# The order table of a hybrid decoder layer, made anew: POOL's transfers, VectorE's rows beside POOL's, and TensorE's fp32 runs

## The chip, the core and the metric

The kernel runs on one core of a Trainium2 chip. Its engines are TensorE (PE in the profile; PEld is its weight load), VectorE (DVE), ScalarE (ACT), GpSimd (POOL) and SyncE (SP, which only issues transfers here). Each engine works through one queue of instructions in order; semaphores hold an instruction until what it needs is there. The metric is the device time of one execution in microseconds; several executions give a median.

## The reference, cut to what matters

One post-norm decoder layer over 512 tokens of width 1024, batch 1, all in float32:

```python
h = x @ w_in[l]
y_a = nsa_attention(nsa_q, cmp_k, cmp_v, ...) @ w_nsa_out[l]     # 8 heads of 64, 2 groups, three branches
y_b = gated_deltanet(gdn_qkv, ...) @ w_gdn_out[l]                # 4 heads of 128, chunks of 64
mix = (sigmoid(gate_a) * y_a + sigmoid(gate_b) * y_b) @ w_o[l]
x = layer_norm(ALPHA * x + mix, ln1_g[l], ln1_b[l])
f = (silu(gate) * val) @ w_down[l]                               # gate, val = split(causal_dwconv(x @ w_up, conv_w))
x = layer_norm(ALPHA * x + f, ln2_g[l], ln2_b[l])
```

The compressed branch of the attention takes a softmax over 31 blocks; the selected and the windowed branch are causal softmaxes over 512 keys. The delta rule needs, for each head and chunk, the inverse of a lower triangular 64 x 64 matrix.

## The kernel before

**Tiling.** Activations lie transposed, 128 channels on the partitions and 512 tokens along the row. Every large product is computed on pairs: an operand is split into a rounded half `h` and the rest `l` (both float32r), and `product` (L484, L486, L487) adds three matmuls of 512 columns for each 128 x 128 block of weights: `xh·wh`, `xl·wh`, `xh·wl`. `split_w` loads the weights (`raw`, L463, on SP), rounds them (`wh`, L470 on ScalarE or L472 on another engine) and subtracts (`wl`, L474). Transposes and the small products of the delta rule's inverse are plain fp32 matmuls, so TensorE's queue changes between fp32 and float32r.

**Stages.** The input projection, the two mixers of eight and of four heads, interleaved, come first (to about 335 us), then the merge with its gates (`merge`, `mt` L1121, `pm` products, L1199 and L1201; to about 440 us), the output projection, and the feed-forward part. The names that are needed below:
- `cmp_attn` (L993 to L1020) makes the compressed branch of a group: the scores `cs`, their exponentials (L1007, four on ScalarE), their sums `csm` (L1009 to L1012), the product `cs<-cs,csm` (L1013, VectorE, both inputs in SBUF), and four transposes of it (L659) on TensorE.
- `scores` (L1035 on) makes one unit of a head: two matmuls (L1042, L1043), the masked minimum (L1046, VectorE), the exponential (L1048, ScalarE), the reciprocal (L1050), then the scaling: for some units VectorE's `mn<-mn,gsig` (L1056, one column) and ScalarE's L1057, for others L1059 on VectorE or POOL. `flip` transposes it (L1075) and multiplies by the values (L1089).
- For each head of the delta rule, `gdn_tri` runs a recurrence of 15 steps on VectorE (`xs`, L772 and L773) that ends in `z` (L775), `gdn_inv` (L784 to L829) builds the inverse out of it by small fp32 matmuls, with copies `x`, `ym` and `z` between them; `gdn_mid` scales columns (`grh`, `grl`, L720, L721, and `at`, L743, POOL). The convolution in front of it makes `acc`, `th`, `kq` and `vraw` (L642 to L655).
- `rsqrt` (L525) is a power of few columns on POOL.
- POOL also issues transfers that add up weights in DRAM: `sums_o` (L503, `osum`, 1024 KB each) and `sums` (L513, `wsum`, 2816 KB each).

**What sets the order.** Code, pools and engine choices create the instructions; at the end, `queues` puts each engine's instructions into the order that the table QUEUES writes out by hand. A number in the table is the place at which the instruction was created on its engine; it comes after the one that stands before it in the table:

```python
    for k, runs in QUEUES.items():
        last = None
        for run in runs.split():
            a, _, b = run.partition("-")
            for n in range(int(a), int(b or a) + 1):
                i = made[k][n]
                if last is not None:
                    tc.add_manual_dep(i, last.name, ...)       # NoSync: a place in the queue, no wait
                last = i
```

Of the kernel before, what the change touches and what calls it, by code (L numbers as in the profile page):

```python
# [70 lines left out]
def layout(a):  # L71
# [62 lines left out]
    "PE": """0-9 11-12 10 13-32 41 38 35-37 33 42-43 53 39 34 54 44-45 47-48 40 50-52 49 55 46 65 56-57 66 59-60 58 61-63 67 64  # L134
71-72 77-78 74 68 79 69 89 75-76 73 70 86 90 87 80 83 91 88 98 81-82 107 101 108 99 84 109-110 100 111 85 102 112 95
113-114 96 115 103 116-117 92 118-119 93 120-122 94 97 123-148 155-178 149-153 104-106 154 183-205 207 206 208-220
179-180 221-230 181-182 235-251 259-260 252-254 261 255 262-264 231 265-267 232 302 268-271 256 303 272 257-258 233
273 234 304-305 274-277 306-307 278-282 308 310 309 311 360 283-290 361 388 291-298 362-365 389-391 366 312-313
367-370 392 371-372 314-315 373-374 393 375-377 394 378 395 379-383 396 299-300 397-405 444-446 301 447 416 406-407
417 408-410 418-419 411 420-434 456 435-436 448-449 457 437-439 458 450 316-317 451 320-321 318 322-323 319 459-463  # L140
324-327 464-466 328 332-339 329-330 467 331 468-471 513 472 340-347 473 514 474-475 348-355 476-477 515 356-359 452
384-387 516 478 517 479 501-502 453-455 412-415 518 503 519-521 504 522-526 440-441 527 442-443 723-724 528-529
725-727 530-532 728-729 480 484 481-483 533-534 485 505-506 535-536 730 486 507-508 731-733 487 734-738 751 739
488-489 752 740 490 509 491 741-742 492 541-542 753 493-494 754 743 495 510 496 543 511 546 755 497 544-545 512 547
756-757 498-499 744 758 500 548 759-760 549-551 560-561 761 745 762-765 562 565-566 766 552 767 746 553 768 554 537
555 591-592 563-564 567 538 568-569 539-540 581-582 769 570 593-596 556 597 557 598 558 599-600 770-771 559 571 583
# [1425 lines left out]
```

## Time and profile before

| | |
|---|---|
| median of three runs (lowest to highest) | 833.2 us (832.77 to 833.51) |
| the profiled execution, its own time | 831.55 us |
| its span, first to last instruction | 829.8 us |
| mean granted clock of TensorE | 0.992 of full speed |
| TensorE busy | 809.2 us, 98% of the span |
| VectorE, ScalarE, POOL busy | 602.5, 409.2, 180.5 us |
| share of the chain that ended last: TensorE, VectorE, DMA | 82%, 9%, 4% |

A row of the profile names the engine, the line of the kernel, the operation and the tiles, `out<-in`. Busy time is the time in which an engine executes something; a wait is the idle time in front of an instruction, with what ended it. The clock of TensorE is given as a share of its full 2.4 GHz.

### The profile page before, as it was taken

The page shows a single profiled execution, that of the slowest core. Times are in us where ns is not written, and L with a number is a line of the kernel's source. Part 1 is how long each engine was busy: PE and PEld are TensorE (multiplying, and loading weights), DVE is VectorE, ACT ScalarE, POOL GpSimd, SP SyncE. Part 2 cuts the span into 40 slices and gives each one's busy share as a digit, 9 for nine tenths or more (in the row PEclk, how much of TensorE's full clock was granted, in tenths as well). Part 3 has the DMA queues.
Part 4 walks back from the last instruction along what each step waited for, and adds up shares of the span by engine and source line. Part 5 has one row for each costly group of instructions (what it writes and reads, how often), then busy time and mean ns, then how long its engine had stood idle before and what let it go on. Part 6 is the DMA issues. An engine that isn't in the chain of part 4 may idle for free.

```text
span 829.8 us, 11767 instructions
## 1 busy us (share of the span) xinstructions
PE 809.2 (98%) x4138; PEld 673.8 (81%) x4138; DVE 602.5 (73%) x1339; ACT 409.2 (49%) x912; POOL 180.5 (22%) x176
## 2 busy tenths in 40 slices
PE   9999899999999999999999999999999999999996
PEld 8778688778888888888788898888888888878784
DVE  5656779979868976647549965667577577687897
ACT  4453487765576764513335333435334344574641
POOL 0333805141266111152200111102112101100001
PEclk9999999999999999999999999999999999999999
DMA  8333615134284711334365476333938932466583
GB/s 279 102 92 101 252 32 133 44 96 108 49 219 111 233 51 52 120 108 128 115 241 177 152 147 211 125 102 102 215 103 249 229 102 80 150 199 182 190 257 124
DMA packets 43979, 119.58 MB, mean 144 GB/s; under 512 B 3472, under 2 KB 4624, under 8 KB 43664
## 3 DMA queue, kind: packets, MB, share of 16 engines
q1 hardware_dynamic: 32144, 87.37, 32.3%
q0 software_dynamic: 11776, 31.46, 16.3%
q8 instruction: 33, 0.54, 0.3%
q14 instruction: 26, 0.21, 0.1%
HBM read 116.72 MB, written 33.55 MB: 181 GB/s over the span
## 4 chain that ended last, share of the span: by engine, by line
PE 82%; DVE 9%; DMA 4%; ACT 2%; issue 2%; POOL 1%; ACTq 0%; DVEq 0%; POOLq 0%; SPq 0%
PE pu L484 10%; PE pu L486 10%; PE pu L487 10%; PE gps L484 8%; PE gps L486 8%; PE gps L487 8%; DMA raw<-wsum 3%; PE pw L1288 3%; PE px L1452 3%; PE pu L1288 2%; PE pz L1452 2%; PE pout L1089 2%; PE pu L1452 2%; PE aps L1075 2%; PE pm L484 2%
## 5 line engine op out<-in xcount | busy, mean ns | idle before, releaser
L474 DVE TENSOR_TENSOR wl<-raw,wh 128x512 fp32r<-128x512 f32 x146 | 102.7, 705 | 78.0 <-ACT wh L470 38.6
L470 ACT ACTIVATE wh<-raw 128x512 fp32r<-128x512 f32 x126 | 79.1, 629 | 133.7 <-PE pu L486 97.0
L486 PE MATMUL pu<-ml,wh 128*128 128x512 f32 (+1 forms) x384 | 131.5, 373 | 0.0
L484 PE MATMUL pu<-mh,wh 128*128 128x512 f32 (+1 forms) x384 | 130.8, 372 | 0.4 <-ACT mh L1267 0.4
L487 PE MATMUL pu<-mh,wl 128*128 128x512 f32 (+1 forms) x384 | 130.8, 373 | 0.0
L484 PE MATMUL gps<-xh,wh 128*128 128x512 f32 x320 | 125.7, 404 | 3.2 <-ACT mt L1121 2.1
L486 PE MATMUL gps<-xl,wh 128*128 128x512 f32 x320 | 126.1, 401 | 0.0
L487 PE MATMUL gps<-xh,wl 128*128 128x512 f32 x320 | 124.4, 400 | 0.0
L484 PEld LDWEIGHTS pu<-mh,wh 128*128 128x128 f32 x384 | 71.3, 188 | 13.4 <-ACT mh L1267 0.7
L487 PEld LDWEIGHTS pu<-mh,wl 128*128 128x128 f32 x384 | 71.4, 188 | 13.0 <-DVE wl L474 0.5
L486 PEld LDWEIGHTS pu<-ml,wh 128*128 128x128 f32 x384 | 71.4, 188 | 12.6
L1410 DVE SCALAR_TENSOR_TENSOR fa<-pu,fcw,fa 128x511 f32<-128x511 f32 (+1 forms) x88 | 64.6, 744 | 17.5 <-ACT fa L1407 16.9
L1416 POOL TENSOR_TENSOR fth<-fth,fa 128x512 f32<-128x512 f32 x22 | 30.4, 1387 | 212.6 <-DVE fth L1415 186.3
L484 PEld LDWEIGHTS gps<-xh,wh 128*128 128x128 f32 x320 | 60.4, 190 | 15.1 <-issue 2.5
L487 PEld LDWEIGHTS gps<-xh,wl 128*128 128x128 f32 x320 | 60.8, 190 | 10.9
L486 PEld LDWEIGHTS gps<-xl,wh 128*128 128x128 f32 x320 | 61.0, 191 | 10.2
L1387 ACT ACTIVATE wh<-raw 128x512 fp32r<-128x512 f32 x67 | 40.1, 626 | 41.0 <-DMA raw<-in_down 13.5
L1388 DVE TENSOR_TENSOR wl<-raw,wh 128x512 fp32r<-128x512 f32 x67 | 44.8, 694 | 17.9 <-ACT wh L1387 17.3
L474 POOL TENSOR_TENSOR wl<-raw,wh 128x512 fp32r<-128x512 f32 x30 | 40.1, 1339 | 13.4 <-ACT wh L470 7.9
L525 POOL TENSOR_TENSOR rs<-rs,minus_half 128x1 f32<-128x1 f32 x8 | 7.2, 901 | 161.4 <-DVE rs L1246 161.4
L1407 ACT ACTIVATE fa<-pu,fcw 128x512 f32<-128x512 f32 x44 | 29.7, 680 | 24.8 <-PE pu L487 22.0
L1048 ACT ACTIVATE sc<-sc,mn 128x384 f32<-128x384 f32 (+2 forms) x64 | 35.7, 560 | 10.5 <-DVE mn L1046 10.1
(365 smaller groups left out, 1719.8 us busy)
## 6 DMA issues: line engine op xcount, KB each, us to landing
raw<-in_up SPq DMA_DIRECT2D x44, 512.0 KB, 3.7
raw<-in_wT SPq DMA_DIRECT2D x40, 512.0 KB, 3.6
wsum<-in_down POOLq DMA_DIRECT2D x6, 2816.0 KB, 20.8
raw<-wsum SPq DMA_DIRECT2D x20, 512.0 KB, 3.9
raw<-in_down SPq DMA_DIRECT2D x15, 512.0 KB, 4.3
osum<-in_wo POOLq DMA_DIRECT2D x6, 1024.0 KB, 9.0
wsum<-wsum POOLq DMA_DIRECT2D x2, 2816.0 KB, 14.6
raw<-in_wm SPq DMA_DIRECT2D x8, 512.0 KB, 3.5
```

Source lines behind the costliest of these rows:

```text
L470: A.activation(wh, r, AF.Copy)
L474: eng.tensor_tensor(wl, r, wh.bitcast(F32), op=OP.subtract)
L484: i = PE.matmul(ps, wh[k], mh_(k), start=(k == 0), stop=False)
L486: PE.matmul(ps, wh[k], ml_(k), start=False, stop=False)
L487: PE.matmul(ps, wl[k], mh_(k), start=False, stop=(k == n - 1))
L1048: A.activation(s[:, i, :n], s[:, i, :n], AF.Exp, scale=-1.0, bias=mn[:, 0, i:i + 1], accum_out=mn[:, 1, i:i + 1])
L1288: PE.matmul(ps[t], a[x](j)[:, ts], w[y][:, j % 2, :], start=fresh and j == 0 and i == 0, stop=j == TT - 1 and i == 2, skip_group_check=True)
L1387: A.activation(hi, raw[:, i], AF.Copy)
L1388: V.tensor_tensor(lo, raw[:, i], hi.bitcast(F32), op=OP.subtract)
L1410: V.scalar_tensor_tensor(acc[:, n:], ps[:, :S - n], w[:, i:i + 1], acc[:, n:], op0=OP.mult, op1=OP.add)
L1416: G.tensor_tensor(th, th, g[1], op=OP.mult)
L1452: m = PE.matmul(ps, a[x][:, j, ts], w[y], start=first and i == 0, stop=last and i == 2, skip_group_check=True)
```

## The change

Only the table QUEUES is replaced. The same instructions run on the same engines with the same tiles; what changes is the place of each in the queue of its engine. The new table was made with a limit on the transfers that POOL has in flight, with VectorE's rows kept from POOL's rows that run back to back, and with fp32 runs of TensorE joined. It is two lines shorter, so each line number of the kernel after it is lower by 2 (L1013 becomes L1011).

```diff
 QUEUES = {
-    "PE": """0-9 11-12 10 13-32 41 38 35-37 33 42-43 53 39 34 54 44-45 47-48 40 50-52 49 55 46 65 56-57 66 59-60 58 61-63 67 64
...
+    "PE": """0-9 11-12 10 13-32 41 38 35-37 33 42-43 53 39 34 54 44-45 47-48 40 50-52 46 49 59 62 55 63 65 56 64 60 66-67 61 57-58
...
```

Of TensorE's 3880 matmuls 1529 keep their place; the others move by up to 48 places forward or 55 back. Counted along the queue, the type changes between fp32 and float32r 337 times to reach an fp32 run where it was 359, that is, 11 runs fewer. From about 600 us (in the times of before) all queues are as they were. On SP a handful of transfers move.

The transfers of POOL: wsum1, which was issued at 268 us, now comes first, behind lo (64.9 us) and ahead of gx (68.1 us); osum1 comes at 81 us (was 97.8), wsum0 at 108 (was 80.6), osum0 and the copy to osum2 at about 219. Two issues, the copy to osum3 and the addition to wsum0, now stand ahead of the score scale sc_3056 (234.2 us). The times are those of the neighbours in the trace of before.

**Place A, POOL's queue at 92 to 104 us.** Before: osum1 is the first sum of output weights, grh and grl belong to the next head of the delta rule, vraw is a convolution's result, wl a weight's rest, vm a copy of 32 rows.

```order
L474 TENSOR_TENSOR wl_1362<-raw_1358,wh_1360 128x512
L643 TENSOR_TENSOR acc_1131<-acc_1131,tap_1137 128x509
L1068 CAST vm_111<-vcb_344 32x128
L652 TENSOR_TENSOR th_1140<-th_1140,acc_1131 128x512
L503 DMA osum1_105<-in_wo 512x1x512
L653 TENSOR_TENSOR vraw_1095<-th_1140,acc_1131 128x512
L474 TENSOR_TENSOR wl_1366<-raw_1358,wh_1364 128x512
L720 TENSOR_TENSOR grh_1539<-cst_320,gdh_339 128x512
L1068 CAST vm_111<-vcb_344 32x128
L721 TENSOR_TENSOR grl_1540<-cst_320,gdl_340 128x512
```

The same places after the change:

```order
L472 TENSOR_TENSOR wl_1362<-raw_1358,wh_1360 128x512
L1066 CAST vm_111<-vcb_344 32x128
L641 TENSOR_TENSOR acc_1131<-acc_1131,tap_1137 128x509
L650 TENSOR_TENSOR th_1140<-th_1140,acc_1131 128x512
L718 TENSOR_TENSOR grh_1539<-cst_320,gdh_339 128x512
L651 TENSOR_TENSOR vraw_1095<-th_1140,acc_1131 128x512
L523 TENSOR_TENSOR rn1_655<-ss_654,minus_half_332 128x4
L719 TENSOR_TENSOR grl_1540<-cst_320,gdl_340 128x512
L472 TENSOR_TENSOR wl_1366<-raw_1358,wh_1364 128x512
L501 DMA osum1_105<-in_wo 512x1x512
```

The osum1 issue is gone from here (it comes earlier); the power row rn1_655 now stands between vraw and grl, and wl_1366 behind grl. On ScalarE the four exponentials of cs stood together in front of th_1140; now the third stands behind x_953 and the fourth behind ym_960, copies that wait for the matmuls dps_948 and dps_955.

**Place A, TensorE's queue.** Before, from the last products of one inverse (dps_955, dps_962) to the transposes of cs_1163; gps_1198 and gps_1368 are products of the input projection, dps_1012 and dps_1081 transposes of kq:

```order
L823 MATMUL dps_955<-z_895,m_826 64x64 x4
L487 MATMUL gps_1198<-xh_93,wl_1196 128x512
L484 MATMUL gps_1198<-xh_93,wh_1194 128x512
L487 MATMUL gps_1368<-xh_93,wl_1362 128x512
L828 MATMUL dps_962<-ym_960,x_953 64x64 x4
L659 MATMUL aps_1178<-ident_322,cs_1163 128x128
L659 MATMUL dps_1012<-ident_322,kq_968 128x128 x4
L484 MATMUL gps_1368<-xh_93,wh_1360 128x512
```

After; dps_962 stands four rows ahead of the first of these, with the four transposes dps_1012 and one matmul gps_1198 between:

```order
L485 MATMUL gps_1198<-xh_93,wl_1196 128x512
L485 MATMUL gps_1368<-xh_93,wl_1362 128x512
L482 MATMUL gps_1368<-xh_93,wh_1360 128x512
L484 MATMUL gps_1368<-xl_94,wh_1360 128x512
L485 MATMUL gps_1368<-xh_93,wl_1362 128x512
L482 MATMUL gps_1368<-xh_93,wh_1360 128x512
L484 MATMUL gps_1368<-xl_94,wh_1360 128x512
L485 MATMUL gps_1368<-xh_93,wl_1362 128x512
L657 MATMUL dps_1081<-ident_322,kq_968 128x128 x3
L657 MATMUL aps_1178<-ident_322,cs_1163 128x128
L657 MATMUL dps_1081<-ident_322,kq_968 128x128
L657 MATMUL aps_1178<-ident_322,cs_1163 128x128
```

Two matmuls of gps_1198, seven of gps_1368 and seven transposes of kq now stand between dps_962 and the first transpose of cs, where there was nothing.

**Place B, POOL's queue at 162 to 172 us.** Before; sc_2258 is a unit of scores, wh_2417 to wl_2423 are the halves of one weight:

```order
L1059 TENSOR_SCALAR sc_1586<-sc_1586,mn_1587,gsig_109 128x384
L643 TENSOR_TENSOR acc_1982<-acc_1982,tap_1987 128x510
L768 COPY xs_3094<-cst_320 128x64
L472 CAST wh_2417<-raw_2415 128x512
L503 DMA osum2_106<-osum1_105 512x512
L472 CAST wh_2421<-raw_2415 128x512
L474 TENSOR_TENSOR wl_2419<-raw_2415,wh_2417 128x512
L743 TENSOR_TENSOR at_1558<-at_1558,cst_320 128x512
L1059 TENSOR_SCALAR sc_2258<-sc_2258,mn_2259,gsig_109 128x256 x2
L474 TENSOR_TENSOR wl_2423<-raw_2415,wh_2421 128x512
```

After:

```order
L1057 TENSOR_SCALAR sc_1586<-sc_1586,mn_1587,gsig_109 128x384
L641 TENSOR_TENSOR acc_1982<-acc_1982,tap_1987 128x510
L1057 TENSOR_SCALAR sc_2258<-sc_2258,mn_2259,gsig_109 128x256
L470 CAST wh_2417<-raw_2415 128x512
L1057 TENSOR_SCALAR sc_2258<-sc_2258,mn_2259,gsig_109 128x256
L472 TENSOR_TENSOR wl_2419<-raw_2415,wh_2417 128x512
L741 TENSOR_TENSOR at_1558<-at_1558,cst_320 128x512
L470 CAST wh_2421<-raw_2415 128x512
L718 TENSOR_TENSOR grh_2133<-cst_320,gdh_339 128x512
L472 TENSOR_TENSOR wl_2423<-raw_2415,wh_2421 128x512
```

The score scales moved ahead of the weights' rows and of at_1558; the copy to osum2 and xs_3094 are gone from here.

**Place C, TensorE's queue at 402 to 407 us.** Before; pm1_4617 is the product on which the merge's next mt waits, gps_4659 the product that waits for the buffer of that mt:

```order
L484 MATMUL pm1_4617<-yoh_4005,wh_4599 128x512
L486 MATMUL pm1_4617<-yol_4036,wh_4599 128x512
L487 MATMUL pm1_4617<-yoh_4005,wl_4601 128x512
L487 MATMUL gps_4566<-xh_93,wl_4564 128x512
L484 MATMUL gps_4659<-xh_93,wh_4651 128x512
```

After:

```order
L485 MATMUL pm1_4617<-yoh_4005,wl_4601 128x512
L485 MATMUL gps_4566<-xh_93,wl_4564 128x512
L482 MATMUL gps_4566<-xh_93,wh_4562 128x512
L484 MATMUL gps_4566<-xl_94,wh_4562 128x512
L485 MATMUL gps_4566<-xh_93,wl_4564 128x512
L482 MATMUL gps_4659<-xh_93,wh_4651 128x512
```

The last matmul of pm1_4617 now has four matmuls of gps_4566 behind it, not one, before gps_4659 begins.

**A later place on POOL**, at 244 to 252 us: kq_2802 (245.8 us) now stands behind an osum issue, a copy and the power row so_2607 (248.15 us), with sc_3171 and wl_2969 behind it as before.

## Rows read from the trace of the kernel before

**Rows 1.** The page, part 1: an engine's busy time, its share of the span, its instructions.

```profile
PE 809.2 (98%) x4138; PEld 673.8 (81%) x4138; DVE 602.5 (73%) x1339; ACT 409.2 (49%) x912; POOL 180.5 (22%) x176
```

**Rows 2.** The list of waits of PE (TensorE) over the whole span: engine, what waits and its line, what ended the wait; us in total, times, longest.

```profile
PE aps L659 <- DVE tiny L578: 3.0, 1, 3.0
PE gps L484 <- ACT mt L1121: 2.1, 1, 2.1
...
PE dps L659 <- DVE z L775: 1.3, 1, 1.3
PE aps L1075 <- ACT sc L1057: 1.1, 1, 1.1
```

**Rows 3.** The table by stretches: from and to in us, length, busy time of each engine (instructions), the granted clock of TensorE as a share of full speed, the DMA engines' busy share, GB/s.

```profile
103.00:106.40 3.40, 3.40 (x15) 3.01 (x13) 0.79 (x4) 1.52 (x7) 0.91 (x1) 0.51 0.28 108
171.20:174.70 3.50, 3.50 (x28) 2.42 (x27) 1.89 (x7) 1.42 (x5) 2.09 (x3) 0.51 0.16 29
406.50:410.20 3.70, 3.70 (x11) 2.87 (x10) 3.24 (x7) 2.08 (x4) 0.00 (x0) 0.54 0.45 146
```

**Rows 4.** The timeline of PE in the second of these stretches: start, duration, engine, line, operation, tiles, shapes, count.

```profile
171.56 0.63 PE L1089 MATMUL pout<-pth,vcat 128*128 128x512 f32 x1
171.99 0.64 PE L1089 MATMUL pout<-ptl,vcat 128*128 128x512 f32 x1
```

**Rows 5.** The timeline of PE a little after the first, at the full clock.

```profile
109.14 0.40 PE L486 MATMUL gps<-xl,wh 128*128 128x512 f32 x1
109.37 0.38 PE L659 MATMUL dps<-ident,vraw 128*128 128x128 f32 x2
...
109.83 0.38 PE L659 MATMUL dps<-ident,vraw 128*128 128x128 f32 x2
...
110.28 0.40 PE L486 MATMUL gps<-xl,wh 128*128 128x512 f32 x1
110.52 0.40 PE L484 MATMUL gps<-xh,wh 128*128 128x512 f32 x1
```

**Rows 6.** The answer on line L1013 (shortest, median and longest duration in ns of its two instructions) and the timeline of DVE (VectorE) at the second.

```profile
L1013 DVE TENSOR_TENSOR cs<-cs,csm x2: 684/2600/4516, 98.1 to 216.3; 128x512 f32<-128x512 f32 x2
...
98.12 4.52 DVE L1013 TENSOR_TENSOR cs<-cs,csm 128x512 f32<-128x512 f32 x1
```

**Rows 7.** The timeline of POOL over the same time.

```profile
98.50 1.35 POOL L653 TENSOR_TENSOR vraw<-th,acc 128x512 f32<-128x512 f32 x1
99.74 1.33 POOL L474 TENSOR_TENSOR wl<-raw,wh 128x512 fp32r<-128x512 f32 x1
100.96 1.11 POOL L720 TENSOR_TENSOR grh<-cst,gdh 128x512 fp32r<-128x512 f32 x1
...
102.86 1.05 POOL L721 TENSOR_TENSOR grl<-cst,gdl 128x512 fp32r<-128x512 f32 x1
```

**Rows 8.** The timeline of PE just before its wait for cs.

```profile
99.04 0.67 PE L828 MATMUL dps<-ym,x 64*64 64x64 f32 x8
```

**Rows 9.** The timeline of ACT (ScalarE) before it.

```profile
95.02 0.69 ACT L1007 ACTIVATE cs<-cs 128x128 f32<-128x128 f32 x3
...
98.26 0.38 ACT L825 ACTIVATE ym<-dps 64x256 f32<-64x256 f32 x1 [0.23 <-PE dps L823]
```

**Rows 10.** The timelines of POOL and of DVE at a power row (line L525) elsewhere.

```profile
253.67 1.05 POOL L525 TENSOR_TENSOR rn<-ss,minus_half 128x4 f32<-128x4 f32 x1 [1.53 <-DVE ss L678]
...
253.77 0.68 DVE L474 TENSOR_TENSOR wl<-raw,wh 128x512 fp32r<-128x512 f32 x1
```

**Rows 11.** The timelines of DVE and of POOL before the second fall of the clock.

```profile
166.25 2.54 DVE L1056 TENSOR_TENSOR mn<-mn,gsig 128x1 f32<-128x1 f32 x2
168.72 0.41 DVE L1046 CUSTOM_DVE_ANT_0 sc<-aps,cst 128x256 f32<-128x256 f32 x1
...
166.19 1.29 POOL L474 TENSOR_TENSOR wl<-raw,wh 128x512 fp32r<-128x512 f32 x1
167.42 1.28 POOL L743 TENSOR_TENSOR at<-at,cst 128x512 f32<-128x512 f32 x1
...
170.95 1.11 POOL L1059 TENSOR_SCALAR sc<-sc,mn,gsig 128x256 f32<-128x256 f32 x2 [2.25 <-DVE mn L1050]
```

**Rows 12.** The timeline of all engines before the third, of which three rows are shown.

```profile
403.41 0.39 PE L487 MATMUL pm<-yoh,wl 128*128 128x512 f32 x1
...
405.35 0.60 ACT L1121 ACTIVATE mt<-gps 128x512 f32<-128x512 f32 x1 [8.61 <-DVE mt L1201]
...
406.09 0.47 PE L484 MATMUL gps<-xh,wh 128*128 128x512 f32 x1 [2.06 <-ACT mt L1121]
```

**Rows 13.** The table by stretches once more, at two other places.

```profile
80.00:90.00 10.00, 10.00 (x55) 8.51 (x56) 7.19 (x27) 5.65 (x12) 7.67 (x7) 1.00 0.90 320
140.00:150.00 10.00, 9.98 (x55) 7.94 (x54) 10.00 (x34) 9.36 (x24) 5.13 (x6) 1.00 0.65 198
```

**Rows 14.** The timelines of POOL and of PE at a later power row.

```profile
248.15 1.03 POOL L525 TENSOR_TENSOR so<-so,minus_half 128x4 f32<-128x4 f32 x1 [1.03 <-DVE so L887]
249.60 0.92 POOL L1059 TENSOR_SCALAR sc<-sc,mn,gsig 128x512 f32<-128x512 f32 x1 [0.41 <-DVE so L889]
250.49 1.29 POOL L474 TENSOR_TENSOR wl<-raw,wh 128x512 fp32r<-128x512 f32 x1
...
252.44 0.39 PE L487 MATMUL gps<-xh,wl 128*128 128x512 f32 x1
```

More of the change, by code (lines that the diff above doesn't have):

```diff
@@ L139 @@
[L139 to L143, printed above, removed]
@@ new lines @@
+1460-1462 1457 1463 1472-1473 1398 1483-1485 1399-1401 1486 1402 1487-1488 1474 1464 1501-1502 1465-1466 1475-1476
+1467 1582 1489 1583 1490 1335 1503 1468 1517-1518 1339-1341 1504 1342 1336-1338 1505-1506 1491-1494 1343-1346
+1519-1520 1469 1495 1521 1470 1347-1348 1522 1351-1358 1349 1471 1507-1508 1350 1509-1511 1496-1499 1512-1513
+1359-1366 1523-1524 1544 1500 1545 1584-1585 1546 1367-1374 1525 1514 1547-1550 1610-1611 1515-1516 1586-1588
+1375-1378 1551 1526 1612-1613 1527 1552-1554 1589 1614 1528 1615 1563-1564 1529-1530 1590 1616 1591-1592 1531-1532
@@ new lines @@
+2850-2852 2835 2853 2836 2854-2860 2866 2837 2867 2861 2868 2838 2869 2862 2870 2839-2840 2871-2874 2863 2875 2864
+2841 2876-2878 2865 2879-2881 2890-2891 2882 2892 2883 2893-2902 2884-2886 2903 2914-2915 2904 2916-2917 2887
+2918-2920 2905 2921 2888 2906 2922-2925 2889 2907-2908 2926 2909 2927 2910 2938 2928 2939-2941 2911 2942-2943
+2912-2913 2944 2929 2945-2950 2930-2931 2951 2962 2932 2963 2952 2964-2965 2953-2954 2933 2966 2955 2967-2968 2934
+2969 2935 2970-2971 2936 2972 2956 2973 2957-2959 2937 2960 2986 2974-2975 2987 2961 2976-2978 2988-2991 2979
@@ new lines @@
+3290-3291 3301 3292 3302-3303 3273 3304-3306 3293-3294 3307 3295 3308 3296 3309-3312 3322 3297 3313-3314 3323 3315
+3324-3330 3316-3317 3331-3332 3318 3333-3335 3319 3336 3320 3346 3337-3338 3347 3339-3342 3348-3349 3343-3344
+3350-3352 3345 3353 3370 3354 3321 3355 3371 3356-3361 3372 3362 3373-3379 3363 3380 3364-3365 3381 3366-3367
+3394-3395 3382 3368 3396 3383 3397-3402 3384 3403 3369 3404 3385-3387 3405 3388-3390 3406 3391 3407 3392 3408
+3418-3419 3409 3420 3393 3421-3424 3427 3410 3428 3411 3429 3425 3412 3426 3413 3430-3431 3433-3434 3414 3435 3432
@@ new lines @@
+3821-3825 3849 3826 3850-3851 3827-3828 3852-3853 3829 3854-3855 3830-3836 3856 3837 3857 3838-3842 3858 3843-3844
+3859 3845-3846 3860-3879""",
+    "DVE": """0 27 104 1-4 6 5 7 9 8 10-11 13 12 14 17 15-16 18 58-60 19 61 22 64 20-21 90 65 23 66 62 31 67 32 63 33 25 34 72 35-36
+73 37-54 74 68-69 83 70-71 84 81 91 82 92 55 93 85-87 94 56 88 95 75 80 151 153 29 152 102 30 76-77 28 154 107 57
+109-110 108 89 164 111 165 112 115 96 113 97 114 166-167 116 79 117 98 118-119 99 120 100 121-122 101 123-126 103 127
@@ new lines @@
+37 140 62 26 41 45 54 48 55 42 36 49 51 47 52 64 66 65 67 46 68 57 69 58 50 53 56 59 61 108 104 63 109 75 60 76 80 92
+88 77 81 87 110 144 90 78 84 71-72 106 86 70 73 93 85 74 94 82 91 95 89 96-99 79 100 83 101 111 102-103 112-130 132
+131 133-137 147 138-139 142 150 143 145 153 148 146 149 151-152 154-155 157 156 160 159 158 161 163 162 165 164
+166-171""",
+    "SP": """0-7 17 8-9 15 25 10 12 11 13-14 19 18 16 20-24 26-75 80 79 81-82 78 83 77 84-85 76 86-134 136-165 167 135 169 171
+173-178 168 179-180 172 182 166 170 181 183-184""",
```

365 lines of the change are left out of this document (171 added, 194 removed).

## The prediction, made before the result was known

> **What bounds the kernel now.** I read the page first: TensorE is busy for 809.2 us of the span of 829.8 us [rows 1]. VectorE, the next, is far below that. So the time can fall only where TensorE waits or runs at a lower clock; work taken from another engine counts only if TensorE stood waiting for it. The list of TensorE's waits comes next [rows 2]. It names few long ones: 3.0 us for a row of VectorE (the releaser shown is the small row L578 that ended last; the tile is cs), 2.1 us for `mt` L1121 in the merge, 1.3 us for `z` L775 and 1.1 us for a scaled score L1057. The table by stretches shows what comes behind three of them: in 103 to 106.4, 171.2 to 174.7 and 406.5 to 410.2 us the granted clock is 0.51, 0.51 and 0.54, that is 1.2 GHz for nearly the whole stretch [rows 3]. Before each fall TensorE had waited: 2.97 us, then 1.3 and 1.1 us within seven, then 2.06 us. At the low level two 512-column matmuls start 0.43 us apart [rows 4], at the full one 0.24 us [rows 5], so 3.4 us at the low level do the work of 1.9 us: each fall costs 1.5 us.
>
> **Place A, 96 to 106 us.** VectorE's `cs<-cs,csm` (L1013) starts at 98.12 and takes 4.52 us; the other of its kind takes 0.68 us [rows 6]. Over the same time POOL runs a DMA issue and then vraw, wl_1366 and grh without a gap, and grl after a short copy [rows 7]. VectorE's row ends where the third of these long rows ends. TensorE has finished L828 by 99.7 [rows 8] and has only the transposes of cs in front of it.
>
> The new order does three things here. On ScalarE, two of the four exponentials that L1009 sums now stand behind x_953 and ym_960, one each; all four were over by 95.7, the copy ym ran from 98.26 to 98.64 [rows 9]. Its matmuls are due some 0.4 us sooner, as two products now stand behind them, so the last exponential ends at 98.4 to 98.9. The sum (0.7 us), the reciprocal and two small products bring cs<-cs,csm to a start of 100.0 to 100.5, later than before. On POOL, th_1140 is followed by grh, vraw, and then the power row rn1_655: with their old durations (1.1 and 1.35 us) the power row runs from about 100.3 to 100.9 for 1.05 us. Beside such a row VectorE is not held: a wl with two SBUF inputs took 0.68 us inside one of 1.05 us [rows 10]. So I take it that cs passes in this opening and ends at 101.0 to 101.9. On TensorE nine 512-column matmuls (9 x 0.23) and seven transposes (7 x 0.11) stand between L828 and the first cs transpose, 2.8 us that fill 98.9 to 101.7. A wait of 0 to 0.3 us is left of 2.97: gain 2.7 us, and as a long wait preceded each fall of the clock, 1.5 us more. **A: 4.2 us.** The bounds are 0 (the opening is missed) and 4.5.
>
> The Trainium skill, "SBUF — State Buffer", section "Who interferes with whom", says that a VectorE instruction with two SBUF inputs and a GpSimd instruction that reads SBUF exclude each other, that the one issued first holds the shared ports for its whole length, and that the order of issue decides. This trace agrees that they exclude each other; it differs on the length, since L1013 waited through several rows of POOL, 4.52 us, not one. By that section alone cs would have ended by about 100.5 before the change (vraw's end at 99.85 and its own 0.68 us), and in the changed kernel the power row, which reads SBUF, would hold it too.
>
> **Place B, 160 to 175 us.** `mn<-mn,gsig` (L1056), rows of one column, stands from 166.25 to 168.79 while POOL runs wl_2419 and at_1558 back to back until 168.70 [rows 11]. Now a score scale (sc_2258, L1059) stands ahead of wh_2417, and a second one ahead of wl_2419 and at_1558. It needs extremes (L1046, from 168.72) that come behind L1056 on VectorE, and ran at 170.95. So POOL stands idle when L1056 comes. The scaled score is then some 2.4 us sooner and TensorE's 1.15 us for it go, with 0.2 us right behind: 1.35 us. The pushed-back wl_2419, at 1.3 us a row, still ends before TensorE's work on the stretch 171 to 175 is over. The wait for z ahead of it stays: nothing that VectorE does before z is removed. Whether the clock falls without the second wait I can't read from any row; I put in half of 1.5. **B: 2.1 us**, bounds 0 and 2.9.
>
> **Place C, 403 to 410 us.** From the start of the last pm matmul, 403.41, the chain L1199, L1201, L1121 takes until 406.09 [rows 12], 2.68 us. One matmul covers it now; four will, so three more, 0.7 us. About 1.5 us of waiting are left. Half of the clock's 1.5 again. **C: 1.4 us**, bounds 0.5 and 2.2.
>
> **Joined runs.** Two fp32 runs of two transposes each and three 512-column matmuls fill 109.14 to 110.28, 1.14 us [rows 5]; 4 x 0.11 and 3 x 0.23 make 1.13. A change of type costs under 0.01 us in such a place; the longest step there, 0.32 us from one matmul to the next run, bounds a join at 0.1 us. For 11 joins I take 0.1 us, bounds 0 and 1.
>
> **Transfers.** wsum1 now goes out at 66 us, osum1 at 81 and wsum0 at 108. The stretch 80 to 90, where wsum0 ran and the DMA engines were busy to 0.90, has TensorE at 10.00 of 10 [rows 13]. The loads of SP's queue lie so far ahead there that a slower one is covered; 0, and where the cover fails some tenths for each load. The two POOL issues now ahead of the score scale sc_3056 (about 231 to 238 us) keep it some 3 us longer; TensorE's use moved back by some 2.6 us. Bounds of that: 0 and 1.
>
> **New waits.** Of the 3880 matmuls over 2000 stand elsewhere, moved by up to 55 places, so rows that were in time need not be. One that I walked: behind the power row so_2607 at 248.15 (1.03 us) now stand kq (1.3), the score scale sc_3171 (0.92) and wl_2969 (1.29), which then ends at 252.7; TensorE wants it at 252.44 less one matmul, 252.2 [rows 14]: 0.5 us. Three such places and a part of the bound at sc_3056 make 1.8 us, my estimate; below it lies 0, above it one more place like C, with its fall of the clock, 2.1 + 1.5 us.
>
> **The sum.** 4.2 + 2.1 + 1.4 + 0.1 - 1.8 = 6.0 us off. The profiled execution took 831.55 us for a span of 829.8 us; it lies 1.65 us under the median of the three runs, 833.2 us, which I take as the base: 833.2 - 6.0 = 827.2 us. The other case inside this mechanism is that the clock falls nowhere and no new wait appears: 4.5 + 2.9 + 2.2 + 0.1 = 9.7, so 823.5 us.
>
> **The rivals.**
> - *The opening at A is missed.* If the power row holds VectorE like any other POOL row, or cs comes as grl starts, cs waits through grl and wl_1366 (1.05 and 1.33 us) to 104.3 and, with the osum1 issue behind them, to 105.2. TensorE then waits 2.6 to 3.5 us instead of 2.97, the clock falls again, and the 2.8 us of pulled-forward products are missing behind cs, whose readers come 1.7 to 2.6 us later than now. Against the other terms (at best 2.1 + 1.4 + 0.1 - 1.8 = 1.8 us off, without the halves for the clock 0.3) that gives 833 to 835.5 us. It decides for slower once cs ends after about 105 us. For it speaks the 4.52 us itself; against it the wl beside the power row. That a power row, which reads SBUF, counts like any other follows from the section of the Trainium skill's "SBUF — State Buffer" named above.
> - *A's gain is lost at z.* In 140 to 150 us VectorE is busy for 10.00 of 10 us [rows 13]. If z came no sooner, TensorE would only wait longer at 164 us: A's 4.2 us are lost and 831.2 us are left, with a further new wait 833. Against it: VectorE itself gets 3.8 us back at A and 2.4 at B.
> - *New waits prevail.* Two or three places of C's size (3.6 us each) among the moved rows between 180 and 400 us: 834 to 838 us. For it speaks how many rows move; against it that the stretches with most slack on the other engines are there.
>
> **Chances and range.** The sum 0.50 (824.5 to 830), its better case 0.14 (822 to 824.5), A's gain lost at z 0.17 (831 to 834), the opening missed 0.10, new waits prevail 0.09. A difference under 0.2%, 1.7 us, cannot be told from none. All of the first two, and a little of z, are faster: 0.67. Most of z and a part of the missed opening are the same: 0.14. The rest is slower: 0.19. The range from 822.5 to 834.0 leaves out about one tenth above and less below; the likeliest case alone is 824.5 to 830.
>
> **What would show it.** In the changed profile: L1013 near 0.7 us and no wait of TensorE over 0.5 us for cs; L1056 at 0.15 us and no wait for L1057 near 167 us; a wait for L1121 near 400 us of about 1.5 us; a granted clock of 1.0 right after the cs transposes. The steps fail if L1013 again takes over 2 us, if the wait for z grows by what A saved, or if a low clock stands behind new waits between 180 and 400 us.

## The result, and the profile after

The changed kernel takes 826.43 us (median of 4, 825.69 to 828.08) where the kernel before took 833.36 us (median of 4, 832.77 to 835.01): a ratio of 0.9927, with a 95% interval of 0.9909 to 0.9946, that is 4.5 to 7.6 us faster. Its profiled execution took 826.54 us for a span of 824.8 us, 5.0 us less than the span before. All its line numbers are lower by 2 than those of before.

The page: TensorE is still the bound, and is busy for 3.3 us less [rows 1].

```profile
span 824.8 us, 11773 instructions
PE 805.9 (98%) x4138; PEld 671.2 (81%) x4138; DVE 601.6 (73%) x1339; ACT 409.7 (50%) x912; POOL 181.6 (22%) x176
```

The list of TensorE's waits (what waits, for what; us in total, times, longest):

```profile
PE dps L791 <- DVE ym L788: 2.4, 1, 2.4
PE gps L482 <- ACT mt L1119: 1.5, 1, 1.5
PE gps L555 <- DVE vm L552: 1.4, 1, 1.4
PE dps L657 <- DVE z L773: 1.1, 1, 1.1
PE gps L482 <- issue: 0.9, 1, 0.9
PE aps L1073 <- DVE sc L1057: 0.9, 1, 0.9
PE dps L737 <- DVE yT L893: 0.7, 1, 0.7
```

Against [rows 2]: the 3.0 us for cs and the 1.1 us for the scaled score of L1057 (now L1055) are gone, the wait for `mt` is 1.5 us, that for z is 1.1. A wait of 2.4 us for `ym` is new and now the longest.

The table by stretches (stretch, its length, busy time and count for PE, PEld, DVE, ACT and POOL, granted clock, DMA share, GB/s) shows what comes behind it. The three low stretches of [rows 3] are gone; one is left, at 218.1 us (the clock is low too behind TensorE's last matmul, in every kernel, where it costs TensorE nothing):

```profile
99.00:103.00 4.00, 4.00 (x24) 3.37 (x23) 3.39 (x8) 3.89 (x18) 4.00 (x4) 1.00 0.00 0
218.10:221.60 3.50, 3.50 (x10) 2.63 (x10) 2.08 (x9) 0.88 (x4) 0.00 (x0) 0.51 0.57 106
```

**Place A.** The timeline (start, duration, engine, line, operation) shows VectorE's row and POOL's beside it:

```profile
98.34 1.28 POOL L651 TENSOR_TENSOR vraw<-th,acc 128x512 f32<-128x512 f32 x1
...
99.58 1.05 POOL L523 TENSOR_TENSOR rn<-ss,minus_half 128x4 f32<-128x4 f32 x1
...
99.90 0.69 DVE L1011 TENSOR_TENSOR cs<-cs,csm 128x512 f32<-128x512 f32 x1
...
100.61 1.23 POOL L719 TENSOR_TENSOR grl<-cst,gdl 128x512 fp32r<-128x512 f32 x1
```

The row that took 4.52 us [rows 6] takes 0.69, inside the power row.

**Place B.** The rows of one column, which took up to 2475 ns, stay under 0.2 us (shortest, median, longest in ns):

```profile
L1054 DVE TENSOR_TENSOR mn<-mn,gsig x30: 150/154/193, 109.6 to 313.7; 128x1 f32<-128x1 f32 x30
```

**The new wait, at 212 us.** The timeline of the three engines:

```profile
211.80 1.20 POOL L501 DMA_DIRECT2D osum<-in_wo  x1
...
212.47 1.16 POOL L470 CAST wh<-raw 128x512 fp32r<-128x512 f32 x1
212.48 4.15 DVE L472 TENSOR_TENSOR wl<-raw,wh 128x512 fp32r<-128x512 f32 x1
213.03 1.82 POOL L741 TENSOR_TENSOR at<-at,cst 128x512 f32<-128x512 f32 x1
214.27 1.80 POOL L472 TENSOR_TENSOR wl<-raw,wh 128x512 fp32r<-128x512 f32 x1
...
216.55 0.41 DVE L788 TENSOR_TENSOR ym<-dps,cst 128x256 f32<-128x256 f32 x1
...
217.11 1.08 PE L791 MATMUL dps<-ym,x 128*128 128x64 f32 x8 [2.43 <-DVE ym L788]
```

It is the picture of place A before the change, at another place: a transfer issued by POOL, three rows of POOL behind it, a VectorE row with two SBUF inputs that starts with them and ends 0.56 us behind the last (4.15 us for a row that takes 0.69 elsewhere), and behind it the copy that TensorE wants. So VectorE is held through all three rows of POOL and does its own work after them. TensorE waits 2.43 us and the clock falls.

### The profile page after: what moved, and what is told of

Read it like the earlier page. It is cut to its first block, busy times and chain, and to the rows that moved or that the text cites. A ratio compares the mean times of both kernels' runs of the same rounds, so it can differ in the third digit from the quotient of the medians.

```text
span 824.8 us, 11773 instructions
## 1 busy us (share of the span) xinstructions
PE 805.9 (98%) x4138; PEld 671.2 (81%) x4138; DVE 601.6 (73%) x1339; ACT 409.7 (50%) x912; POOL 181.6 (22%) x176
## 4 chain that ended last, share of the span: by engine, by line
PE 86%; DVE 6%; DMA 3%; ACT 2%; issue 1%; SPq 1%; POOL 0%; DVEq 0%; ACTq 0%
PE pu L484 10%; PE pu L482 10%; PE pu L485 10%; PE gps L482 9%; PE gps L484 9%; PE gps L485 8%; PE px L1450 5%; PE pz L1450 3%; PE pout L1087 2%; PE aps L1073 2%; PE pm L484 2%; PE pm L482 2%; PE pm L485 2%; PE pu L1450 2%; PE dps L657 1%; PE pw L1286 1%
## 5 line engine op out<-in xcount | busy, mean ns | idle before, releaser
L472 DVE TENSOR_TENSOR wl<-raw,wh 128x512 fp32r<-128x512 f32 x146 | 105.8, 728 | 74.0 <-PE pu L485 33.4
L1386 DVE TENSOR_TENSOR wl<-raw,wh 128x512 fp32r<-128x512 f32 x67 | 44.8, 694 | 19.1 <-ACT wh L1385 18.5
```

The source lines that it names most:

```text
L472: eng.tensor_tensor(wl, r, wh.bitcast(F32), op=OP.subtract)
L1386: V.tensor_tensor(lo, raw[:, i], hi.bitcast(F32), op=OP.subtract)
```

## The experiments

Unless said otherwise, each starts from the changed kernel and moves rows of one queue. The ratio is to the kernel before, timed beside it.

| kernel | median us (lowest to highest, n) | ratio, 95% |
|---|---|---|
| changed kernel | 826.43 (825.69 to 828.08, 4) | 0.9927, 0.9909 to 0.9946 |
| a_row_moved | 822.64 (822.27 to 824.41, 4) | 0.9890, 0.9865 to 0.9916 |
| a_no_cover | 829.24 (824.16 to 832.86, 10) | 0.9943, 0.9914 to 0.9972 |
| b_scores_behind | 828.71 (826.14 to 830.24, 8) | 0.9951, 0.9934 to 0.9968 |
| c_cover_back | 828.88 (824.71 to 832.4, 10) | 0.9952, 0.9929 to 0.9975 |
| fix_dve | 822.60 (821.85 to 823.33, 4) | 0.9881, 0.9859 to 0.9904 |
| fix_two | 822.16 (820.37 to 823.10, 4) | 0.9876, 0.9849 to 0.9903 |
| before_b (from before) | 832.54 (829.79 to 835.89, 10) | 0.9994, 0.9969 to 1.0018 |
| transfers_back | 829.11 (827.0 to 830.04, 7) | 0.9958, 0.9943 to 0.9973 |
| before_no_issue (from before) | 825.26 (824.13 to 827.18, 4) | 0.9910, 0.9878 to 0.9942 |
| issue_212 | 822.49 (821.45 to 823.44, 4) | 0.9870, 0.9835 to 0.9905 |
| runs_split | 827.39 (821.68 to 829.26, 10) | 0.9923, 0.9895 to 0.9952 |
| best | 822.28 (821.6 to 823.07, 4) | 0.9867, 0.9850 to 0.9885 |

### The power row taken out of place A (a_row_moved)

```diff
 L501 DMA osum_105<-in_wo 512x1x512
+L523 TENSOR_TENSOR rn_655<-ss,minus_half 128x4
 L472 TENSOR_TENSOR wl<-raw,wh 128x512
...
 L651 TENSOR_TENSOR vraw<-th,acc 128x512
-L523 TENSOR_TENSOR rn_655<-ss,minus_half 128x4
 L719 TENSOR_TENSOR grl<-cst,gdl 128x512
```

> The changed kernel with one row of POOL's queue moved: the power row rn1_655 goes back to where it was (behind the osum1 issue at 79 us), so that vraw, grl, wl_1366 and an osum1 issue run without it between. Theory (the opening at the power row is what frees VectorE): cs<-cs,csm, 0.69 us in the changed kernel, takes 2 to 4 us again, TensorE waits 0.6 to 2.6 us at the first cs transpose (none there in the changed kernel), and the time rises from 826.4 us by 0.6 to 4.1 us, the upper end if the clock falls to 1.2 GHz again. Rival (the 2.8 us of matmuls put ahead of the transposes are what saved the wait, and VectorE loses to one POOL row at most): cs ends by about 101.4 us, no wait, the time stays within 0.5 us of 826.4.

The opening is gone and cs meets grl and wl back to back. The timeline of place A and of 212 us:

```profile
98.84 1.05 POOL L719 TENSOR_TENSOR grl<-cst,gdl 128x512 fp32r<-128x512 f32 x1
99.85 1.27 POOL L472 TENSOR_TENSOR wl<-raw,wh 128x512 fp32r<-128x512 f32 x1
99.95 1.72 DVE L1011 TENSOR_TENSOR cs<-cs,csm 128x512 f32<-128x512 f32 x1
...
212.25 1.20 POOL L501 DMA_DIRECT2D osum<-in_wo  x1
212.90 0.69 DVE L472 TENSOR_TENSOR wl<-raw,wh 128x512 fp32r<-128x512 f32 x1
212.92 1.16 POOL L470 CAST wh<-raw 128x512 fp32r<-128x512 f32 x1
```

cs waits for one row of POOL, 1.72 us, and TensorE 0.95 us, with no fall of the clock. The power row is worth about 1 us of wait here, not the whole of A's gain. The kernel is still faster than the changed one, which nothing expected: at 212 us VectorE's wl now starts 0.02 us ahead of POOL's row instead of 0.01 us behind it, takes 0.69 us, and the wait for `ym` is gone. A step of some hundredths decides a place worth nearly 4 us.

### The cover at place A taken away (a_no_cover)

```diff
 L826 MATMUL dps<-ym,x 64x64 x4
+L657 MATMUL aps<-ident,cs 128x128
 L657 MATMUL dps<-ident,kq 128x128 x3
...
-L657 MATMUL dps<-ident,kq 128x128 x3
-L657 MATMUL aps<-ident,cs 128x128
-L657 MATMUL dps<-ident,kq 128x128
+L657 MATMUL dps<-ident,kq 128x128 x4
```

> The changed kernel with the first cs transpose moved back to where it stood, right behind the last matmul of dps_962 (98.4 us); POOL, VectorE and ScalarE as in the changed kernel. Theory (the opening alone is worth part of the gain, the cover the rest): cs still ends at about 100.6 us in 0.7 us, TensorE waits some 2.1 us, no longer than 2.4, and the time rises by 2.1 us, or by 3.6 with a fall of the clock. Rival (the cover is not needed): a rise under 0.5 us.

cs takes 0.69 us as before, but its first transpose stands right behind dps_962. TensorE's waits and the table by stretches:

```profile
PE aps L657 <- DVE cs L1011: 2.2, 1, 2.2
```

```profile
99.90:103.30 3.40, 3.02 (x10) 2.58 (x11) 1.10 (x2) 1.23 (x6) 3.40 (x4) 0.50 0.00 0
219.30:226.20 6.90, 5.91 (x19) 4.95 (x19) 4.64 (x17) 0.88 (x4) 0.00 (x0) 0.51 0.60 112
```

The wait of 2.2 us and the low clock of A are back. The median is 2.8 us above the changed kernel's, the ratio 0.0016 (1.3 us) higher with overlapping intervals; the wait shows the cover's worth more sharply than the times. The profiled execution took 831.2 us, and the ten spread from 824.2 to 832.9, so what it shows need not happen in each. Matmuls pulled forward between dps_962 and cs carried 2.2 us of A's gain. The second row shows that a low stretch can last 6.9 us.

### The scores put back behind the rows of place B (b_scores_behind)

```diff
-L1057 TENSOR_SCALAR sc<-sc,mn,gsig 128x256
 L470 CAST wh<-raw 128x512
-L1057 TENSOR_SCALAR sc<-sc,mn,gsig 128x256
 L472 TENSOR_TENSOR wl<-raw,wh 128x512
 L741 TENSOR_TENSOR at<-at,cst 128x512
+L1057 TENSOR_SCALAR sc<-sc,mn,gsig 128x256 x2
```

> The changed kernel with the two score scales of sc_2258 on POOL moved behind at_1558, so that wh_2417, wl_2419 and at_1558 come ahead of them as before the change. Theory (POOL's rows back to back held the one-column row L1056): the one-column row takes over 1 us again at about 160 to 163 us, TensorE gets a wait of about 1.1 us for a scaled score, and the time rises by 1.4 us, or by 2.9 with a fall of the clock to 1.2 GHz. Rival (the place was won by the other moved rows): no change within 0.5 us.

Inconclusive. With nothing ahead of them that waits, wl and at ran from 149.5 to 152.1 us, long before the row they were to meet; the longest L1054 stayed at 193 ns. The ratio is 0.0024 above the changed kernel's, with overlapping intervals. TensorE has two waits for scores (1.3 us at 152.4 and 1.1 us at 156.4). The first comes from another meeting: VectorE's scaling of that score (L1057) starts at 150.83 us, 0.02 us after POOL's at, and takes 1.46 us where the shortest of its kind takes 0.48.

### The same move made in the kernel before (before_b)

```diff
 L768 COPY xs<-cst 128x64
+L1059 TENSOR_SCALAR sc<-sc,mn,gsig 128x256 x2
 L472 CAST wh<-raw 128x512
 L503 DMA osum_106<-osum_105 512x512
...
 L743 TENSOR_TENSOR at<-at,cst 128x512
-L1059 TENSOR_SCALAR sc<-sc,mn,gsig 128x256 x2
```

> The kernel before with only POOL's two rows sc_2258 moved ahead of wh_2417, wl_2419 and at_1558. Theory (those rows, back to back, held L1056 for 2.4 us): L1056 takes 0.15 to 0.2 us at 166 us, TensorE's wait of 1.15 us for the scaled score goes, the clock either falls behind it or not: 1.3 to 2.9 us off the time of before. Rival (other rows of the new table made the gain at place B): L1056 over 1 us, or the wait stays, and the time is that of before.

Every L1056 is now at most 161 ns and the 1.1 us for L1057 are gone; the move frees L1056, as B has it. But a wait of 2.0 us for the next scaled score appears at 177.7 us, with a fall of the clock behind it, and the time is that of before. Nothing is gained by the move alone. The timeline of POOL and VectorE ahead of that wait shows why:

```profile
170.32 0.70 POOL L503 DMA_DIRECT2D osum<-osum  x1
...
172.82 1.26 POOL L743 TENSOR_TENSOR at<-at,cst 128x512 f32<-128x512 f32 x1
173.00 3.90 DVE L474 TENSOR_TENSOR wl<-raw,wh 128x512 fp32r<-128x512 f32 x1
174.05 1.29 POOL L474 TENSOR_TENSOR wl<-raw,wh 128x512 fp32r<-128x512 f32 x1
175.31 1.04 POOL L720 TENSOR_TENSOR grh<-cst,gdh 128x512 fp32r<-128x512 f32 x1
```

The copy to osum2 is still issued here, and POOL's rows follow it without a gap. Another row of VectorE, a wl, is held through three of them, and the score that TensorE wants is scaled behind it.

### The three products of place C put back (c_cover_back)

```diff
+L485 MATMUL gps<-xh,wl 128x512
+L482 MATMUL gps<-xh,wh 128x512
+L484 MATMUL gps<-xl,wh 128x512
 L485 MATMUL pm_4617<-yoh,wl 128x512
-L485 MATMUL gps<-xh,wl 128x512
-L482 MATMUL gps<-xh,wh 128x512
-L484 MATMUL gps<-xl,wh 128x512
```

> The changed kernel with one matmul moved: the last one of pm1_4617 goes back to one row ahead of gps_4659's start, as before the change. Theory: the wait for mt L1119 near 402 us grows from 1.47 to about 2.15 us, and that is long enough for the clock to fall to 1.2 GHz for 3.4 us, as before: the time rises by 0.7 + 1.5 = 2.2 us. Rival (the fall does not hang on this wait's length): a rise of 0.7 us and a granted clock of 1.0 behind it.

TensorE's waits and the stretch behind:

```profile
PE gps L482 <- ACT mt L1119: 2.7, 1, 2.7
```

```profile
402.70:409.60 6.90, 6.20 (x15) 4.88 (x16) 3.96 (x10) 3.33 (x7) 0.00 (x0) 0.51 0.24 78
```

The wait grows from 1.47 to 2.67 us and the clock falls where it had not; the median is 2.4 us higher, with overlapping intervals of the ratio, and the profiled execution is the longest of the ten. Of the 1.2 us the cover is some 0.7, three matmuls of 0.23 us. The rest is a meeting that the move brought about: VectorE's L1199, which took 0.69 us at 400.65, now starts at 401.27, beside POOL's wl, and takes 1.36 us.

### VectorE's wl at 212 us placed earlier (fix_dve), and place C covered more (fix_two)

```diff
 L771 TENSOR_TENSOR xs<-xs,tmp 128x4
+L472 TENSOR_TENSOR wl<-raw,wh 128x512
 L910 TENSOR_TENSOR kl<-gps,kh 64x512 x2
-L472 TENSOR_TENSOR wl<-raw,wh 128x512
```

> The changed kernel with one row of VectorE's queue moved: the wl_2807 subtraction that took 4.15 us at 212.48, behind POOL's DMA issue, rounding, at and wl rows, now stands two rows earlier, behind the last xs step, before POOL's z, issue and rows have begun. Theory (the same meeting of rows that cost 4.5 us at place A has come up at 212 us, and it makes TensorE's new wait of 2.43 us and the one fall of the clock that is left): that row takes about 0.7 us, the wait for ym at 217 us falls below 0.6 us, no low clock in 216 to 222, and the time falls from 826.4 by 2.0 + 1.5, to about 823 us. Rival (POOL's rows only meet another of VectorE's rows there, kl or ym): a wait over 1.5 us stays and the time stays within 1 us of 826.4.

wl now runs at 210.71 us, ahead of the issue, in 0.69 us; the wait for `ym` and the low clock are gone and 3.8 us with them. That is what the meeting at 212 us costs.

fix_two has this move and, at C, three pm matmuls ahead of gps_4566 instead of among its products.

> The run before this one and, at place C, three matmuls moved: the last one of pm0_4603 and the last two of pm1_4617 stand ahead of the nine of gps_4566, so that nine and not four matmuls cover the chain to mt L1119. Theory: the chain takes 2.7 us as it did, so the wait at 402 us falls from 1.47 to about 0.5 us; with the other move about 822 us. Rival (the chain L1197, L1199, L1119 is held by something else than the pm product): the wait stays over 1.2 us.

The wait for `mt` falls to 1.1 us only: the chain behind pm is now held on VectorE, whose L1199 takes 1.23 us beside POOL's wl rows. No difference to fix_dve can be told.

### POOL's transfers put back to their old neighbours (transfers_back)

All 16 issues stand behind the row that preceded each in the kernel before (its lines are 3 below those of before); at A:

```diff
 L650 TENSOR_TENSOR th_1140<-th_1140,acc_1131 128x512
+L501 DMA osum1_105<-in_wo 512x1x512
 L718 TENSOR_TENSOR grh_1539<-cst_320,gdh_339 128x512
...
 L472 TENSOR_TENSOR wl_1366<-raw_1358,wh_1364 128x512
-L501 DMA osum1_105<-in_wo 512x1x512
```

> The changed kernel with all sixteen transfers that POOL issues put back behind the rows that they followed before the change (wsum0 at about 78 us, osum1 at 95, wsum1 at 263, and so on); nothing else moved. Theory (the limit on the transfers is worth nothing by itself, since the loads run ahead; what their issues do is to lengthen POOL's row of work): the loads on SP stay within 0.5 us of their landing times, TensorE gets no wait for a load, and the time moves by the meetings of VectorE and POOL alone, at most by one wait and one fall of the clock either way (-4 to +4 us), with the wait for ym at 217 us changed if the issue ahead of it is gone. Rival (three transfers at once slow the loads): a wait of TensorE or of the rounding rows for raw, and over 4 us more.

The timeline of POOL and of VectorE's cs at A:

```profile
97.61 0.75 POOL L500 DMA_DIRECT2D osum<-in_wo  x1
98.26 1.17 POOL L717 TENSOR_TENSOR grh<-cst,gdh 128x512 fp32r<-128x512 f32 x1
99.26 1.41 POOL L650 TENSOR_TENSOR vraw<-th,acc 128x512 f32<-128x512 f32 x1
100.50 1.16 POOL L522 TENSOR_TENSOR rn<-ss,minus_half 128x4 f32<-128x4 f32 x1
...
100.97 3.49 DVE L1010 TENSOR_TENSOR cs<-cs,csm 128x512 f32<-128x512 f32 x1
101.53 1.15 POOL L718 TENSOR_TENSOR grl<-cst,gdl 128x512 fp32r<-128x512 f32 x1
102.54 1.36 POOL L471 TENSOR_TENSOR wl<-raw,wh 128x512 fp32r<-128x512 f32 x1
...
104.52 0.33 PE L656 MATMUL aps<-ident,cs 128*128 128x128 f32 x1 [2.70 <-DVE cs L1010]
```

The power row is there, and cs starts inside it; still it takes 3.49 us and ends behind the two rows that follow. TensorE waits 2.70 us and the clock falls. What differs in POOL's order from the changed kernel at this place is the issue at 97.61. In exchange no issue stands ahead of the rows at 212 us: VectorE's wl (218.22 us here) takes 1.77 us and the wait for `ym` is gone. The median is 2.7 us above the changed kernel's, with intervals that just overlap. The loads of SP between 200 and 300 us land later (4.7 us, 3.5 in the changed kernel), but TensorE waits for none.

### The two issues alone moved in the kernel before (before_no_issue)

```diff
 L652 TENSOR_TENSOR th<-th,acc 128x512
-L503 DMA osum_105<-in_wo 512x1x512
 L653 TENSOR_TENSOR vraw<-th,acc 128x512
 L474 TENSOR_TENSOR wl<-raw,wh 128x512
...
 L721 TENSOR_TENSOR grl<-cst,gdl 128x512
+L503 DMA osum_105<-in_wo 512x1x512
...
 L472 CAST wh<-raw 128x512
-L503 DMA osum_106<-osum_105 512x512
 L472 CAST wh<-raw 128x512
...
 L474 TENSOR_TENSOR wl<-raw,wh 128x512
+L503 DMA osum_106<-osum_105 512x512
```

> The kernel before with two transfers of POOL moved and nothing else: the osum1 issue (97.78 us) goes behind grl, the copy to osum2 (164.93 us) behind wl_2423. POOL's long rows stay back to back at places A and B. Theory 1, as in the prediction (rows back to back hold VectorE, whatever stands ahead of them): cs<-cs,csm still takes over 3 us, L1056 over 2 us, and the time is that of before. Theory 2, new (a transfer that POOL has just issued makes its following rows keep VectorE out; without one, VectorE loses to one row at most): cs takes 0.7 to 2 us, L1056 under 1.5 us, TensorE's wait for cs falls from 2.97 us to 0 to 1.2 us and the time falls by 2 to 6 us.

POOL's rows stand as back to back as they did. The timeline of both places:

```profile
97.62 1.30 POOL L653 TENSOR_TENSOR vraw<-th,acc 128x512 f32<-128x512 f32 x1
97.81 1.66 DVE L1013 TENSOR_TENSOR cs<-cs,csm 128x512 f32<-128x512 f32 x1
98.88 1.72 POOL L474 TENSOR_TENSOR wl<-raw,wh 128x512 fp32r<-128x512 f32 x1
...
160.73 1.28 POOL L474 TENSOR_TENSOR wl<-raw,wh 128x512 fp32r<-128x512 f32 x1
161.47 1.79 DVE L1056 TENSOR_TENSOR mn<-mn,gsig 128x1 f32<-128x1 f32 x2
161.98 1.26 POOL L743 TENSOR_TENSOR at<-at,cst 128x512 f32<-128x512 f32 x1
```

cs waits to the end of vraw, passes, and POOL's wl waits for it in turn (1.72 us for 1.3): VectorE loses to one row. So does each L1056 at B (0.56 and 1.31 us). TensorE has no wait for cs left, and the clock is low only at C. Two issues moved in the kernel before give 7.1 us, as much as the whole new table.

### The issue at 212 us moved in the changed kernel (issue_212)

```diff
 L773 TENSOR_TENSOR z<-xs,cst 128x512
-L501 DMA osum_106<-in_wo 512x1x512
 L470 CAST wh<-raw 128x512
 L741 TENSOR_TENSOR at<-at,cst 128x512
 L472 TENSOR_TENSOR wl<-raw,wh 128x512
+L501 DMA osum_106<-in_wo 512x1x512
```

> The changed kernel with one of POOL's transfers moved: the addition to osum2, issued at 211.8 us between z and wh_2875, goes behind wl_2877. VectorE's queue is the changed one; wh, at and wl stay back to back. Theory 1 (rows back to back): VectorE's wl_2807 still takes over 2.5 us and TensorE's wait for ym stays over 1 us. Theory 2 (the issue): it takes 0.7 to 2 us, the wait for ym is under 0.6 us and the clock does not fall there; about 823 us instead of 826.4.

```profile
212.76 1.27 POOL L741 TENSOR_TENSOR at<-at,cst 128x512 f32<-128x512 f32 x1
212.84 1.75 DVE L472 TENSOR_TENSOR wl<-raw,wh 128x512 fp32r<-128x512 f32 x1
213.99 1.73 POOL L472 TENSOR_TENSOR wl<-raw,wh 128x512 fp32r<-128x512 f32 x1
```

VectorE's wl starts 0.08 us after POOL's at, waits for that row alone, takes 1.75 us instead of 4.15, and gets in ahead of the next. There is no wait for `ym` and no low clock here, and the kernel takes 3.9 us less.

All fourteen traces (the kernel before, the changed one and the twelve experiments) agree with this. Compare each VectorE row with the shortest of its line and shape in its trace, and call a run of POOL's rows unbroken where no gap in it is over 0.1 us. Eleven rows took 1.7 to 3.8 us more than the shortest, and each of them stood in an unbroken run with an issue earlier in it, 0.3 to 4.4 us ahead. Where no issue was ahead, the most was 1.2 us, about one row of POOL, also in a run of nine rows (162.9 to 171.0 us in the changed kernel). One row of VectorE shows both: the scaling of a score beside POOL's grh, wl and grl, first in the changed kernel, then in transfers_back, where the copy to osum2 was issued at 168.74 us and the rows behind it have no gap.

```profile
168.39 1.68 DVE L1057 TENSOR_SCALAR sc<-sc,mn,gsig 128x384 f32<-128x384 f32 x1
...
173.15 3.40 DVE L1056 TENSOR_SCALAR sc<-sc,mn,gsig 128x384 f32<-128x384 f32 x1
```

So VectorE's time of arrival within a row of POOL is not what decides between one row and the whole run: held rows came up to 0.61 us after the start of the row that they met (at place A before, ahead of it), rows that passed after one came 0.05 to 0.84 us after it. Nor is every row behind an issue held: in transfers_back a wl of VectorE at 177.49 us takes 0.68 us inside a power row that follows an issue at 176.29.

### The joined runs cut again (runs_split)

39 fp32 runs of TensorE were cut by one 512-column matmul each, so that the type changes to fp32 413 times, not 337.

> The changed kernel with 39 fp32 runs of TensorE cut open: at each, the outermost transpose changes places with the 512-column matmul next to it, so that the type changes 413 times along the queue instead of 337 (38 runs more; the change joined 11). Theory (a join is worth 0.01 to 0.02 us): the time rises by 0.4 to 0.8 us, too little to tell. Rival (up to 0.1 us for each): it rises by 3.8 us, so that the change's 11 joins would have been worth 1.1 us.

The times spread from 821.7 to 829.3 us and can't tell. In the profiled execution VectorE came 0.03 us ahead of POOL at 212 us and passed; whether it lost there in the longer ones no record shows. Their mean granted clock, 0.993 to 0.996 for the six over 827 us against 0.996 to 0.998 for the four under 824, would fit a fall of the clock. Set beside issue_212 in the traces, a cut costs 0.003 us (median), so by this estimate the 11 runs saved by the change are worth some 0.03 us.

### Both places mended (best)

issue_212 with the order of fix_two carried further at C: both pm tiles ahead of gps_4566.

> The changed kernel with the addition to osum2 moved behind wl_2877, as in issue_212, and at place C the last products put in the order pm0, pm1, gps_4566, so that nine matmuls cover the chain to mt L1119 and pm0 ends earlier. Theory: no wait for ym at 215 us and no low clock before the end, as there; the wait for mt at 400 us falls from 1.47 to under 0.6 us: about 821.5 us, 1 us under issue_212. Rival (VectorE's L1199, two inputs in SBUF, meets POOL's wl there again, as in fix_two, where it took 1.23 us): the wait stays near 1 us and the time near 822.3 us.

The timeline at C:

```profile
394.84 2.96 POOL L472 TENSOR_TENSOR wl<-raw,wh 128x512 fp32r<-128x512 f32 x2
395.19 1.49 DVE L1199 TENSOR_TENSOR mt<-mt 128x512 f32<-128x512 f32 x1
```

The wait for `mt` is 0.99 us, because L1199 now meets a row of POOL. Four versions, issue_212, fix_dve, fix_two and this one, lie within 0.5 us of each other, at a ratio of 0.987 to 0.988: they beat the kernel before by 10 to 11 us and the changed one by about 4, and can't be told apart.

## Why the prediction was right, and which steps were not

The total, 827.2 us forecast and 826.43 measured, is inside the range and faster, as held likeliest. That it came so close is luck: the gains at A, B and C were put 1.7 us too low together, the new waits some 3 us too low, and these errors stand against each other. One of the signs of failure that the prediction named came true, a low clock behind a new wait between 180 and 400 us. By the profiled executions (span 5.0 us shorter, forecast 6.0):

- **A, forecast 4.2, got 4.5.** The wait of 2.97 us is gone and no low clock follows. cs started at 99.90 (forecast 100.0 to 100.5) and passed inside the power row, as said. The cover carried what a_no_cover put back, 2.2 us; it was needed because the new order on ScalarE starts cs 1.8 us later than before. In before_no_issue, without that order, TensorE has no cover and no wait for cs of 0.2 us or more. What failed is the reason: the step that held rows back to back to be what keeps VectorE out. In before_no_issue the rows are as close and cs takes 1.66 us; in transfers_back the opening is there and cs takes 3.49. What the traces tie it to is an issue ahead in POOL's unbroken run of rows. The change moved osum1 away from A, and I had priced that at nothing.
- **B, forecast 2.1, got 2.85.** The 1.35 us went as worked out, and the clock did not fall: 1.5 us instead of half. Again the osum2 copy, which had stood 1.3 us ahead of the row at 166.25, is gone from there too; before_b (its rows moved) and before_no_issue (the issue moved) each free L1056 alone, so the change had two sufficient causes for that and this study doesn't share the gain between them. With the issue left in place, though, the move gained no time: in before_b the holding passed to the next row of VectorE.
- **C, forecast 1.4, got 2.1.** A wait of 1.5 us was forecast and 1.47 measured, so the cover was worth what was said. No fall followed it, so the clock's share is whole, not half.
- **Joins, forecast 0.1, got 0.03** by runs_split.
- **Transfers, forecast 0: the step that failed.** The loads were covered, as said; but an issue has a price on POOL's own queue, in how it shuts VectorE out of the rows behind it. It was looked for in the loads, and on POOL only as time, at sc_3056.
- **New waits, forecast 1.8, got about 5.** The walked place at 251 us gave none of 0.2 us or more. Instead the osum2 addition put at 211.8 us made a new meeting of the same kind, 2.43 us of wait and 1.5 of clock; 0.7 us for `yT` at 193 us, 0.3 more for a score at 154.5 and up to 0.5 at 449 are the rest. The bound "one more place like C with its fall of the clock" had the size, not the place. A forecast by the rule that before_no_issue shows would have found it in the order: an issue, three rows, and a wl of VectorE.
- The sum of these, 9.5 off and about 5 on, leaves 4.5 of the 5.0 us; the remaining half microsecond isn't assigned.
- **The rivals.** The opening was not missed. The price of missing it was wrong, too: in a_row_moved, without the power row, cs waits for one row and TensorE for 0.95 us, not for 2.6 to 3.5. A's gain was not lost at z: its wait is 1.08 us where it was 1.3. New waits took about half of the gain, but at one place, not two or three.

The Trainium skill, "SBUF — State Buffer", section "Who interferes with whom", has the instruction that issued first hold the ports for its whole length. The trace agrees where no transfer was just issued: VectorE waits for one row and then passes (1.66, 1.72, 1.75 us), and POOL's next row waits for it. It differs behind an issue, where VectorE was held through up to three rows (4.52, 4.15, 3.49 us), and at the power row, beside which cs took its plain 0.69 us. It differs in the order at place A before the change as well, where the prediction took vraw as the first: cs starts at 98.12, vraw at 98.50 [rows 6], [rows 7], and cs is held all the same. The same section says that DMA does not contend with a compute engine, and sets apart only a transfer whose descriptors GpSimd makes, which VectorE can hold up. Here the effect runs the other way: the issue makes POOL's next rows hold VectorE up. Whether the transfer's bytes matter no run here shows.
